# A hybrid S5 / RG-LRU encoder block: chunk matrices begun earlier and summed by accumulating transfers, a first norm by halves, half tiles for the embedding's results

## The chip, the cores and the metric

The kernel runs on one core of one Trainium2 chip. The metric is device time in microseconds of one execution, all inputs and outputs in HBM. The core has a matrix engine (PE), a vector engine (DVE), a scalar engine (ACT), GpSimd (POOL), a queue engine that issues transfers (SP) and 16 DMA engines. All of the engines run in order, each through its own list of instructions, and wait for each other by semaphores.

## The reference, cut to what matters

One layer on 1024 tokens of 1024 channels in float32. The part that the change touches is the S5 branch: `u_a`, the first 1024 columns of the in-projection, goes through a complex diagonal state space in 64 groups of 16 channels with 64 states, forwards and backwards, and a GELU.

```python
u = rms_norm(h, g_mix[l])
proj = u @ w_in[l]
u_a, x_b, gate_b, merge_a, merge_b = jnp.split(proj, SPLITS, axis=-1)
...
lam_bar = jnp.exp(lam * dt)
b_bar = ((lam_bar - 1.0) / lam)[..., None] * lax.complex(b_re, b_im)
bu = jnp.einsum('bsgh,gph->bsgp', u.astype(jnp.complex64), b_bar)
state = linear_scan(a, bu, reverse)
return jnp.einsum('bsgp,ghp->bsgh', state, c).real
...
gate_p = jax.nn.sigmoid(rms_norm(h, g_ple[l]) @ w_ple_gate[l])
h = h + gate_p * (p[l] @ w_ple_proj[l])
```

Around it stand an RG-LRU branch, a merge of both branches, an output projection `w_o`, a SwiGLU feed-forward layer of 2816 columns, and the gated embedding of the last two lines above.

## The kernel before

Every float32 product is made of three passes over pieces `h` and `l` (high and low part) of both operands: `gemm` (L159) multiplies wh·xh, wh·xl and wl·xh into one PSUM bank, 128x512 a matmul. `split` (L134, L135) makes the pieces of a weight: a cast on ACT, a subtraction on DVE.

The kernel runs through these stages, by the times of the profile:

- **First norm and transposes**, to 24 us (L190 to L221). `norm_pair` squares two tiles of 128 tokens on ACT (L194), makes their reciprocal root with two small Newton chains on DVE, and scales them (L198); then `transposed_half` transposes four tiles through PSUM (tiles `ptx`) into `xh` and `xl`, which hold the channels on the partitions.
- **In-projection of `u_a`** (`pi_u`) and the tables of the S5 part, to about 143 us.
- **The S5 stage**, to about 510 us: 16 chunks `hb` of 64 channels, `s5_step` (L635). For a chunk, `s5_mats` (L487) loads a table `tb` and makes two matrices of 128x1024 by products of broadcast columns. `mo` and `mt` are each a product, a second product goes to `mu`, and a third row adds it (L503 twice, L505). Then PE multiplies `mo` and `mt` into the PSUM tile `pk` (L516, L519); ACT copies `pk` to `kt` (L522, L523), DVE adds the skip term (L526), and `kt` goes through HBM to a matrix `m0`. PE also transposes `mt` into `pmi` (L536), which ACT copies to `mi` (L538). `s5_front` multiplies the chunk's inputs `U` by `mi` into `pS` (L551) and rotates the result into `bb`. `s5_mid` scans `bb` on DVE (L586), carries sums between blocks (tile `carry`), scans again (L610) and rotates the result into the states `X` (L614). `s5_out` multiplies `m0`·U, `mo`·X into `py` (L625 to L627) and stores its GELU.
- In the same stage the in-projections `pi_x`, `pi_g`, `pi_b`, `pi_a` (48 matmuls each) are written behind the steps by `FILL`, and PE takes them while a chunk waits.
- **LRU and branches, merge, `w_o`**, to about 1090 us; then **the feed-forward layer**, whose products `q` (L1060) are recombined by blocks and whose operand sums `s` come from weights `fu` and `ws_fg` (L1047, L1071, L982). Near 1146 us `embed_proj` (L1171) multiplies the embedding by `w_ple_proj` as filler, eight times into two banks `ppj`, copies them into one 128x1024 tile `prj` and stores it to HBM. Down projection, gate and final norm follow.

What sets the order: the program is written as Python loops, and a scheduler of the framework then puts the instructions of each engine in an order, by priority and by the time at which it thinks their operands are ready. The pools take part in this, since a tile waits for the last reader of the buffer that it gets. In the S5 stage these are: `mo` three buffers, `mt` one, `mu` one, `X` two; two PSUM buffers shared by `pk`, `pmi`, `pS` and `py`; two PSUM buffers for the `pi` tiles. Tiles from `ot` (L78) share three buffers of 128x1024: `junk`, the outputs `oi` of the in-projection, `prj`, the operand tiles of the feed-forward sums among them. 128x512 tiles of the tag `vt` have four.

`s5_step` makes matrices and fronts of chunks 0 and 1 first, then, at each step, `s5_mid` of the chunk, `s5_mats` and `s5_front` of the chunk two ahead, and `s5_out` of the chunk.

Of the kernel before, what the change touches and what calls it, by code (L numbers as in the profile page):

```python
# [53 lines left out]
def block_kernel(tc, a, out):  # L54
# [20 lines left out]
    def psb(name):  # L75
        return pb.tile([128, 1024], F32, name=name, tag="pb")
# [112 lines left out]

    def norm_pair(q):  # L190
        qs = slice(q * 2, q * 2 + 2)
        for j in range(q * 2, q * 2 + 2):
            junk = ot("junk")
            A.activation(junk, xt[j], AF.Square, bias=warm, accum_out=ss[:, j:j + 1])  # L194
        A.activation(rs[:, qs], ss[:, qs], AF.Sqrt, bias=epsc, scale=1.0 / D)
        rstd_newton(rs[:, qs], ss[:, qs], nt[:, qs])
        for j in range(q * 2, q * 2 + 2):
            V.tensor_scalar(xt[j], xt[j], rs[:, j:j + 1], None, MUL)  # L198

    def transposed_half(h):  # L200
# [3 lines left out]
        for k0 in range(0, KT, len(ks)):  # L204
# [5 lines left out]
            for k in ks:  # L210
# [3 lines left out]
                V.scalar_tensor_tensor(xl[k0 + k][:, cs], src, g, xh[k0 + k][:, cs].bitcast(F32), MUL, SUB)  # L214

    pv = psb("pv")
    T.transpose(pv[:, :8], grow, ident[:8, :8])
    V.tensor_copy(gmix, pv[:, :8])
    for h in range(2):
        norm_pair(2 * h)  # L220
        norm_pair(2 * h + 1)  # L221
        first_w[h] = split(first_w[h], [128, 8, 128], f"u{h}")
        transposed_half(h)


# [258 lines left out]
    def st5(name, bufs, shape=None):  # L484
        return s5p.tile(shape or [128, 1024], F32, name=name, tag=name, bufs=bufs)

    def s5_mats(hb):  # L487
        tb = tabp.tile([128, MATW], F32, name="tb", tag="tb", bufs=2)
# [10 lines left out]
        def gen(o1, o2, q1, q2, name):  # L499
            t = st5(name, 3 if name == "mo" else 1, [128, 8, 16, 8])  # L500
            u = st5("mu", 1, [128, 8, 16, 8])
            for dst, o, q in ((t, o1, q1), (u, o2, q2)):
                V.tensor_tensor(dst, v8(o).unsqueeze(2).to_broadcast([128, 8, 16, 8]),  # L503
                                v16(q).unsqueeze(3).to_broadcast([128, 8, 16, 8]), MUL)
            V.tensor_tensor(t, t, u, ADD)  # L505
            return t

        mo = gen(O_LA, O_LB, O_K1, O_K2, "mo")
        t = gen(O_T1, O_T2, O_B1, O_B2, "mt")

        k1 = v16(O_K1)
        pk = psb("pk")
# [4 lines left out]
        for g in range(4):  # L517
            for q in (g, 4 + g):
                T.matmul(pk[0:16, g * 128 + 112:(g + 1) * 128], bq[q], k1[:, q, :], start=(q < 4), stop=(q >= 4))  # L519
        kt = tabp.tile([16, 15, 4, 16], F32, name="kt", tag="kt", bufs=1)  # L520
        pkv = pk[0:16].rearrange("p (q n) -> p q n", q=8)
# [110 lines left out]

    sts = {}

    def s5_step(hb):  # L635
        if hb == 0:
            for q in range(2):
                sts[q] = {"m": s5_mats(q)}
            s5_front(0, sts[0])
            s5_front(1, sts[1])  # L640
        s5_mid(hb, sts[hb])
        if hb + 2 < 16:
            sts[hb + 2] = {"m": s5_mats(hb + 2)}
            s5_front(hb + 2, sts[hb + 2])
        s5_out(hb, sts.pop(hb))

# [251 lines left out]
    def half(n):  # L898
        return slice(n * 512, n * 512 + 512)
# [271 lines left out]
    def embed_proj(m):  # L1171

        if m % 4 == 0:
            with hp(HPW):
                wpp[0] = wload(a["w_ple_proj"][0][:, m * 128:m * 128 + 512], f"pp{m}")
        ps = [bank("ppj"), bank("ppj")]
        gemm(ps, wpp[0], pth, ptl, ms=slice((m % 4) * 128, (m % 4 + 1) * 128))
        yield
        t = ot("prj")
        for n in range(2):  # L1180
            A.copy(t[:, half(n)], ps[n])
        dma(prd[m], t)
        yield
# [198 lines left out]
```

## Time and profile before

| | us |
|---|---|
| median of three runs | 1907.72 |
| the three runs | 1906.96, 1907.72, 1909.06 |
| profiled execution, its own time | 1907.41 |
| its span in the trace | 1905.2 |
| PE busy | 1841.4 (97%) |
| DVE busy | 1315.1 (69%) |
| ACT busy | 909.7 (48%) |
| POOL busy | 7.8, 60 instructions |
| granted clock of PE, mean | 0.994 |

The span is the first to the last instruction of the trace; the execution's own time is 2.2 us more. PE idles 63.8 us of the span. A row of a timeline gives start, duration, engine, line of the kernel, operation, tile written and tiles read, shape, and in brackets the idle time of that engine just before the row with what ended it. Consecutive rows of a pipelined engine overlap a little, so that their spacing and not their duration is what one of them adds to a queue.

### The profile page before, as it was taken

To read this page: it belongs to the slowest core of one execution; us is meant where nothing else is said; L and a number is where in the kernel's file an instruction comes from. 1 tells how busy PE (TensorE), PEld (TensorE's weight loads), DVE (VectorE), ACT (ScalarE), POOL (GpSimd) and SP (SyncE) were. 2 spreads that over 40 slices of the span, in tenths; PEclk is the share of its full clock that TensorE was granted. 3 is DMA by queue.
4 is the path that set the end of the run, shared out by engine and by line. 5 is a ranking of instruction groups with operands and counts; after the bars stand their busy time and mean duration, and the time that the engine had idled before them with its cause. 6 is when DMAs were issued, how large, how long until landed. Compare 5 with 4: busy or idle time off the path is not lost.

```text
span 1905.2 us, 23270 instructions
## 1 busy us (share of the span) xinstructions
PE 1841.4 (97%) x8997; PEld 1532.0 (80%) x8997; DVE 1315.1 (69%) x1810; ACT 909.7 (48%) x1238; POOL 7.8 (0%) x60
## 2 busy tenths in 40 slices
PE   7999889988999999999999999999999999999998
PEld 6787777777788888878888887888888888888887
DVE  7517999999534779797444677867777774343875
ACT  6675666656555687865223454223232332122543
POOL 0000000000000000000000000000000000000000
PEclk8999999999999999999999999999999999999999
DMA  4795343433233356565746645422222264322433
GB/s 146 194 234 151 112 128 119 131 115 109 97 111 99 129 193 211 164 210 179 230 134 180 184 166 188 145 76 91 76 92 74 93 217 130 96 83 67 139 111 127
DMA packets 285855, 263.48 MB, mean 138 GB/s; under 512 B 32688, under 2 KB 244784, under 8 KB 285744
## 3 DMA queue, kind: packets, MB, share of 16 engines
q1 hardware_dynamic: 285744, 261.99, 44.2%
q8 instruction: 71, 1.16, 0.3%
q14 instruction: 40, 0.33, 0.1%
HBM read 185.86 MB, written 76.09 MB: 137 GB/s over the span
## 4 chain that ended last, share of the span: by engine, by line
PE 68%; DVE 2%; DMA 1%; ACT 1%; issue 1%; DVEq 0%; ACTq 0%
PE q L1060 22%; PE pfd L159 13%; PE pwo L159 5%; PE ppg L159 5%; PE pi_a L159 5%; PE pgl L159 5%; PE pg L159 4%; PE pbo L159 4%; PE pi_b L159 3%; PE pao L159 2%; PE ppj L159 1%; DMA ld_yb<-ybd 1%; DMA brd<-ta 1%; PE pfin L1312 0%; PE pxr L1195 0%
## 5 line engine op out<-in xcount | busy, mean ns | idle before, releaser
L1271 DVE TENSOR_TENSOR h<-h,pfd 128x512 f32<-128x512 f32 x48 | 32.6, 684 | 113.3 <-PE pfd L159 113.3
L982 ACT CAST s<-rs 128x512 fp32r<-128x512 f32 x44 | 27.2, 618 | 148.4 <-DVE rs L1072 148.4
L159 PE MATMUL pfd<-fh,wh_fd 128*128 128x512 f32 x288 | 88.7, 389 | 0.0
L159 PE MATMUL pfd<-fl,wh_fd 128*128 128x512 f32 x288 | 88.7, 389 | 0.0
L159 PE MATMUL pfd<-fh,wl_fd 128*128 128x512 f32 x288 | 88.6, 389 | 0.0
L134 ACT CAST wh_fd<-ws_fd 128x768 fp32r<-128x768 f32 x24 | 20.1, 835 | 122.1 <-PE pfd L159 121.4
L1060 PE MATMUL q<-xt2h,s 128*128 128x512 f32 x176 | 59.2, 398 | 4.3 <-ACT s L982 3.9
L159 PEld LDWEIGHTS pfd<-fl,wh_fd 128*128 128x128 f32 x288 | 54.1, 188 | 11.3
L159 PEld LDWEIGHTS pfd<-fh,wh_fd 128*128 128x128 f32 x288 | 54.1, 188 | 11.2
L159 PEld LDWEIGHTS pfd<-fh,wl_fd 128*128 128x128 f32 x288 | 54.1, 188 | 11.2
L1060 PE MATMUL q<-xt3h,s 128*128 128x512 f32 x176 | 57.7, 389 | 0.0
L1060 PE MATMUL q<-xt1h,s 128*128 128x512 f32 x176 | 57.7, 389 | 0.0
L1060 PE MATMUL q<-xt4h,a 128*128 128x512 f32 x176 | 57.7, 389 | 0.0
L1060 PE MATMUL q<-xb1h,s 128*128 128x512 f32 x176 | 57.7, 389 | 0.0
L551 PE MATMUL pS<-U,mi 128*128 128x128 f32 x256 | 32.6, 281 | 22.6 <-ACT mi L538 22.6
L551 PEld LDWEIGHTS pS<-U,mi 128*128 128x128 f32 x256 | 29.7, 191 | 28.9 <-ACT mi L538 28.5
L159 PE MATMUL pwo<-mh,wh_wo 128*128 128x512 f32 x128 | 51.5, 402 | 0.0
L159 PE MATMUL ppg<-uh,wh_pg 128*128 128x512 f32 x128 | 50.8, 397 | 0.0
L159 PE MATMUL pwo<-mh,wl_wo 128*128 128x512 f32 x128 | 50.1, 392 | 0.0
L159 PE MATMUL ppg<-uh,wl_pg 128*128 128x512 f32 x128 | 49.9, 390 | 0.0
L159 PE MATMUL ppg<-ul,wh_pg 128*128 128x512 f32 x128 | 49.8, 389 | 0.0
L159 PE MATMUL pwo<-ml,wh_wo 128*128 128x512 f32 x128 | 49.8, 389 | 0.0
(544 smaller groups left out, 5362.9 us busy)
## 6 DMA issues: line engine op xcount, KB each, us to landing
ws_fg<-in_w_ff_gate_dram SPq DMA_DIRECT2D x22, 512.0 KB, 4.2
fu<-in_w_ff_up_dram SPq DMA_DIRECT2D x22, 512.0 KB, 4.0
hid<-up SPq DMA_DIRECT2D x22, 512.0 KB, 3.4
hid<-hid SPq DMA_DIRECT2D x22, 512.0 KB, 4.6
ws_fd<-in_w_ff_down_dram SPq DMA_DIRECT2D x24, 384.0 KB, 3.5
ws_wo<-in_w_o_dram SPq DMA_DIRECT2D x16, 512.0 KB, 5.0
ws_pg<-in_w_ple_gate_dram SPq DMA_DIRECT2D x16, 512.0 KB, 3.9
tb<-tab SPq DMA_DIRECT2D x16, 384.0 KB, 3.1
```

The lines of the kernel that those rows point to most:

```text
L134: A.copy(wh, st)
L159: T.matmul(pn_[:, sub], ww[:, k0 + k, ms], xn[:, sub], start=(first and i == 0), stop=(last and i == tot - 1))
L551: T.matmul(pS[:, q * 128:(q + 1) * 128], mi[:, q, :], rhs, start=True, stop=True)
L982: A.copy(h, raw)
L1060: T.matmul(ps, ww[:, k], xx, start=i == 0, stop=i == 11)
L1271: V.tensor_tensor(hres[m][:, half(n)], hres[m][:, half(n)], ps[n], ADD)
```

## The change

There are three parts.

**S5 matrices.** `s5_mats` is split. Its loads and products become `s5_gens`, which is called for the chunk three ahead of the step (L635 of before, `s5_step`); what is left of `s5_mats` gets the finished tiles. The row on DVE that added `mu` to `mo` or `mt` (L505) is taken out. In its place GpSimd issues a transfer from `mu` to `mo` or `mt`, SBUF to SBUF, 512 KB, whose write adds to what is there (32 in all). `mu` gets two buffers. `kt` becomes a tile of the shared `ot` buffers in place of one of its own. In a step `s5_out` now stands after `s5_mats` and ahead of the next `s5_gens` and `s5_front`.

**First norm.** `norm_half` takes four tiles at once. The squares of the odd tiles move to DVE, one scaling in four moves to ACT. The zero that the second half's squares use is made from a column of `xl[4]`, so that they can't begin earlier.

**Embedding.** The result of `embed_proj` goes through two 128x512 tiles of the tag `vt`, each with its own store, and no longer through one `ot` tile.

```diff
-    def norm_pair(q):
-        qs = slice(q * 2, q * 2 + 2)
-        for j in range(q * 2, q * 2 + 2):
+    def norm_half(h, start):
+
+        qs = slice(h * 4, h * 4 + 4)
+        for j in range(h * 4, h * 4 + 4):
             junk = ot("junk")
-            A.activation(junk, xt[j], AF.Square, bias=warm, accum_out=ss[:, j:j + 1])
+            if j % 2:
+                V.tensor_tensor_reduce(junk, xt[j], xt[j], 1.0, start, MUL, ADD, ss[:, j:j + 1])
+            else:
+                A.activation(junk, xt[j], AF.Square, bias=start, accum_out=ss[:, j:j + 1])
...
-        for j in range(q * 2, q * 2 + 2):
-            V.tensor_scalar(xt[j], xt[j], rs[:, j:j + 1], None, MUL)
+        for j in range(h * 4, h * 4 + 4):
+            if j % 4 == 3:
+                A.mul(xt[j], xt[j], rs[:, j:j + 1])
+            else:
+                V.tensor_scalar(xt[j], xt[j], rs[:, j:j + 1], None, MUL)
...
-        norm_pair(2 * h)
-        norm_pair(2 * h + 1)
+        norm_half(h, zeros[h])
         first_w[h] = split(first_w[h], [128, 8, 128], f"u{h}")
         transposed_half(h)
+        if h == 0:
+
+            V.tensor_scalar(zeros[1], xl[4][:, 0:1].bitcast(F32), 0.0, None, MUL)
...
-    def s5_mats(hb):
+    def s5_gens(hb):
...
             t = st5(name, 3 if name == "mo" else 1, [128, 8, 16, 8])
-            u = st5("mu", 1, [128, 8, 16, 8])
+            u = st5("mu", 2, [128, 8, 16, 8])
...
-            V.tensor_tensor(t, t, u, ADD)
+
+            G.dma_start(out=t.rearrange("p a b c -> p (a b c)"), in_=u.rearrange("p a b c -> p (a b c)"), accum_op=ADD)
             return t
...
-
-        k1 = v16(O_K1)
+        return rb, mo, t, v16(O_K1)
+
+    def s5_mats(hb, rb, mo, t, k1):
...
-        kt = tabp.tile([16, 15, 4, 16], F32, name="kt", tag="kt", bufs=1)
+        kt = ot("kt")[0:16, 0:960].rearrange("p (m g h) -> p m g h", m=15, g=4)
...
         if hb == 0:
-            for q in range(2):
-                sts[q] = {"m": s5_mats(q)}
-            s5_front(0, sts[0])
-            s5_front(1, sts[1])
+            for q in range(3):
+                g = s5_gens(q)
+                if q < 2:
+                    sts[q] = {"m": s5_mats(q, *g)}
+                    s5_front(q, sts[q])
+            gens.append(g)
         s5_mid(hb, sts[hb])
         if hb + 2 < 16:
-            sts[hb + 2] = {"m": s5_mats(hb + 2)}
+            sts[hb + 2] = {"m": s5_mats(hb + 2, *gens.pop())}
+        s5_out(hb, sts.pop(hb))
+        if hb + 3 < 16:
+            gens.append(s5_gens(hb + 3))
+        if hb + 2 < 16:
             s5_front(hb + 2, sts[hb + 2])
-        s5_out(hb, sts.pop(hb))
...
-        t = ot("prj")
         for n in range(2):
-            A.copy(t[:, half(n)], ps[n])
-        dma(prd[m], t)
+            t = qp.tile([128, 512], F32, name="prj", tag="vt", bufs=4)
+            A.copy(t, ps[n])
+            dma(prd[m][:, half(n)], t)
```

The order of the instructions moves with this at three places. In the orders below `xN` is the count of equal instructions in a row, and a number behind a name tells tiles of one name apart.

**PE, the first chunks of the S5 stage.** `pi_x` are in-projections, `pk`, `pmi` and `pS` as above. Before, from the first chunk's `pk`:

```order
L516 MATMUL pk<-mo,mt 16x112 x8
L519 MATMUL pk<-tb,mt 16x16 x8
L536 MATMUL pmi<-ident,mt 128x128 x8
L159 MATMUL pi_x_2044<-xh_118,wh_in_x_2040 128x512 x2
L159 MATMUL pi_x_2044<-xl_126,wh_in_x_2040 128x512 x2
L159 MATMUL pi_x_2044<-xh_118,wl_in_x_2041 128x512 x2
```

And in the changed kernel, from the first chunk's `pk` to the third's:

```order
L531 MATMUL pk<-mo,mt 16x112 x8
L534 MATMUL pk<-tb,mt 16x16 x8
L551 MATMUL pmi<-ident,mt 128x128 x8
L566 MATMUL pS<-U,mi 128x128 x8
L531 MATMUL pk<-mo,mt 16x112 x8
L534 MATMUL pk<-tb,mt 16x16 x8
L551 MATMUL pmi<-ident,mt 128x128 x8
L566 MATMUL pS<-U,mi 128x128 x8
L531 MATMUL pk<-mo,mt 16x112 x8
L534 MATMUL pk<-tb,mt 16x16 x8
L551 MATMUL pmi<-ident,mt 128x128 x8
L159 MATMUL pi_x_2046<-xh_118,wh_in_x_2042 128x512 x2
```

Before, 19 matmuls of `pi_x` stood behind the first `pmi`, 5 and 15 around the first `pS` (which took two chunks at once), and 16 and 5 around the third `pmi`; now none stands until the third chunk's `pmi`.

**DVE, a step in the middle of the stage.** Rows L564 and L565 are rotations, `wl_in_g` is a weight's low part. Before:

```order
L503 TENSOR_TENSOR mo<-tb 128x1024
L602 SCALAR_TENSOR_TENSOR carry<-carry 128x64
L505 TENSOR_TENSOR mo<-mo,mu 128x1024
L607 TENSOR_TENSOR carry<-carry,rb 128x16x7
L503 TENSOR_TENSOR mu<-tb 128x1024
L608 TENSOR_TENSOR carry<-carry 128x8x7
L505 TENSOR_TENSOR mt<-mt,mu 128x1024
L609 TENSOR_TENSOR bb<-bb,carry 128x8x7
L524 TENSOR_TENSOR kt<-ident,dcol 16x64
L610 SCALAR_TENSOR_TENSOR Y<-dzf,bb 128x1024
```

And in the changed kernel:

```order
L514 TENSOR_TENSOR mu<-tb 128x1024
L601 SCALAR_TENSOR_TENSOR Y<-dzf,bb 128x1024
L579 TENSOR_TENSOR risw<-risw,rb 128x1024
L514 TENSOR_TENSOR mo<-tb 128x1024
L580 TENSOR_TENSOR bb<-pS,rb 128x1024
L614 TENSOR_TENSOR carry<-carry,rb 128x128
L584 TENSOR_TENSOR bb<-bb,risw 128x1024
L615 TENSOR_TENSOR carry<-carry 128x64
L135 TENSOR_TENSOR wl_in_g_3370<-ws_in_g_3367,wh_in_g_3369 128x1024
L617 SCALAR_TENSOR_TENSOR carry<-carry 128x64
L514 TENSOR_TENSOR mu<-tb 128x1024
```

The two additions are gone, and the products stand between the rows of other chunks. On POOL, where before only the memsets of `carry`, `dzf` and `X` (L583, L580, L613) stood, two accumulating transfers a step now stand between them, most often `mo` ahead of `carry` and `dzf`, and `mt` ahead of `X`.

**SP, the transfers around the embedding.** `prd` is the store of `prj`, `fu` a weight of the feed-forward layer. Before:

```order
L1182 DMA prd_7740<-prj 128x1024
L1106 DMA hdd_7734<-hd 128x1024
L1106 DMA hdd_7735<-hd 128x1024
L1106 DMA hdd_7736<-hd 128x1024
L1182 DMA prd_7741<-prj 128x1024
L1047 DMA fu_8999<-in_w_ff_up_dram 128x8x128
```

And in the changed kernel:

```order
L1203 DMA prd_7728<-prj 128x512 x2
L1068 DMA fu_8997<-in_w_ff_up_dram 128x8x128
L1140 DMA ru<-hdd_7720 128x1024
L1203 DMA prd_7729<-prj 128x512 x2
```

The load of `fu` now stands behind the fourth result's store and ahead of the fifth's; before, it stood behind the fifth's and three stores of `hd`.

## Rows read from the trace of the kernel before

**Rows 1.** The page's first part: busy time, share, instructions of each engine.

```profile
PE 1841.4 (97%) x8997; PEld 1532.0 (80%) x8997; DVE 1315.1 (69%) x1810; ACT 909.7 (48%) x1238; POOL 7.8 (0%) x60
```

**Rows 2.** What PE waited for: total us, times, longest.

```profile
PE pS L551 <- ACT mi L538: 22.6, 14, 1.9
PE pk L516 <- DVE mt L505: 9.6, 11, 2.2
```

**Rows 3.** Busy time by stretch: length, then each engine; PEclk; DMA share; GB/s.

```profile
core 0: us, PE busy (x) PEld busy (x) DVE busy (x) ACT busy (x) POOL busy (x), PEclk, DMA share, GB/s
...
143.00:163.00 20.00, 17.83 (x82) 14.53 (x81) 10.76 (x10) 9.16 (x10) 0.00 (x0) 1.00 0.77 212
163.00:213.00 50.00, 46.25 (x314) 39.24 (x314) 46.27 (x52) 31.59 (x41) 0.44 (x3) 1.00 0.40 123
213.00:467.00 254.00, 228.64 (x1556) 197.21 (x1557) 246.35 (x278) 160.80 (x229) 5.37 (x37) 1.00 0.39 118
467.00:510.00 43.00, 37.89 (x227) 32.48 (x226) 30.36 (x33) 24.69 (x34) 0.54 (x3) 1.00 0.26 81
```

**Rows 4.** Timeline of PE in one step, from one chunk's pk to the next's.

```profile
277.25 1.69 PE L516 MATMUL pk<-mo,mt 128*16 128x112 f32 x16 [0.94 <-DVE mt L505]
278.78 0.67 PE L519 MATMUL pk<-tb,mt 128*16 128x16 f32 x16
279.38 1.09 PE L536 MATMUL pmi<-ident,mt 128*128 128x128 f32 x8
...
284.42 2.05 PE L551 MATMUL pS<-U,mi 128*128 128x128 f32 x16 [1.65 <-ACT mi L538]
...
298.77 1.69 PE L516 MATMUL pk<-mo,mt 128*16 128x112 f32 x16 [0.96 <-DVE mt L505]
```

**Rows 5.** Timeline of DVE in the same step: the additions.

```profile
293.70 1.19 DVE L505 TENSOR_TENSOR mo<-mo,mu 128x1024 f32<-128x1024 f32 x1
...
297.40 1.22 DVE L505 TENSOR_TENSOR mt<-mt,mu 128x1024 f32<-128x1024 f32 x1
```

**Rows 6.** Timeline of ACT in the same step.

```profile
280.68 1.05 ACT L482 COPY rosw<-Y 64x1024 f32<-64x1024 f32 x1
281.75 0.98 ACT L522 COPY kt<-pk 16x448 f32<-16x448 f32 x1
282.53 0.98 ACT L523 COPY kt<-pk 16x448 f32<-16x448 f32 x1
283.32 1.04 ACT L538 COPY mi<-pmi 128x1024 f32<-128x1024 f32 x1
```

**Rows 7.** Timeline of DVE and PE where the stage begins.

```profile
156.90 1.22 DVE L503 TENSOR_TENSOR mt<-tb 128x1024 f32<-128x1024 f32 x1
158.04 1.22 DVE L505 TENSOR_TENSOR mo<-mo,mu 128x1024 f32<-128x1024 f32 x1
...
159.70 0.62 PE L159 MATMUL pi_x<-xl,wh_in_x 128*128 128x512 f32 x2
160.15 0.61 PE L159 MATMUL pi_x<-xh,wl_in_x 128*128 128x512 f32 x2
162.93 1.69 PE L516 MATMUL pk<-mo,mt 128*16 128x112 f32 x16 [2.17 <-DVE mt L505]
```

**Rows 8.** The page's DMA issues: count, KB each, median us to landing.

```profile
hid<-up SPq DMA_DIRECT2D x22, 512.0 KB, 3.4
ws_wo<-in_w_o_dram SPq DMA_DIRECT2D x16, 512.0 KB, 5.0
...
x<-in_x_dram SPq DMA_DIRECT2D x8, 512.0 KB, 8.1
```

**Rows 9.** Timelines at the embedding: SP's queue, then PE.

```profile
1150.70 0.41 SPq L1182 DMA_DIRECT2D prd<-prj  x1
1151.77 0.38 SPq L1047 DMA_DIRECT2D fu<-in_w_ff_up_dram  x1
...
1160.36 0.50 PE L1060 MATMUL q<-xt2h,s 128*128 128x512 f32 x1 [3.86 <-ACT s L982]
```

**Rows 10.** Timelines of the start: DVE, then PE.

```profile
11.77 1.23 DVE L135 TENSOR_TENSOR wl_u<-ws_u,wh_u 128x1024 fp32r<-128x1024 f32 x1 [0.24 <-ACT wh_u L134]
...
13.90 1.42 DVE L198 TENSOR_SCALAR x<-x,rs 128x1024 f32<-128x1024 f32 x2
...
21.13 0.83 PE L208 MATMUL ptx<-ident,x 128*128 128x128 f32 x4 [4.46 <-DVE xl L214]
```

More of the change, by code (lines that the diff above doesn't have):

```diff
@@ L214, in transposed_half @@
                 V.scalar_tensor_tensor(xl[k0 + k][:, cs], src, g, xh[k0 + k][:, cs].bitcast(F32), MUL, SUB)
+    zeros = [warm, cp.tile([128, 1], F32, name="zero2")]
     pv = psb("pv")
@@ L633, in block_kernel @@
     sts = {}
+    gens = []
     def s5_step(hb):
         if hb == 0:
-            for q in range(2):
-                sts[q] = {"m": s5_mats(q)}
-            s5_front(0, sts[0])
-            s5_front(1, sts[1])
+            for q in range(3):
[4 more added lines that the diff above has]
+            gens.append(g)
         s5_mid(hb, sts[hb])
         if hb + 2 < 16:
-            sts[hb + 2] = {"m": s5_mats(hb + 2)}
+            sts[hb + 2] = {"m": s5_mats(hb + 2, *gens.pop())}
[3 more added lines that the diff above has]
+        if hb + 2 < 16:
             s5_front(hb + 2, sts[hb + 2])
-        s5_out(hb, sts.pop(hb))
     xbd = [dram(f"xbd{f}", [128, 1024]) for f in range(8)]
```

## The prediction

> **What bounds the kernel now.** I read the busy times first, then what PE waited for, then the stretches, then timelines of the stretches in which PE idles. PE is busy 1841.4 us of a span of 1905.2 us [rows 1], so at most 63.8 us can be won without taking matmuls away, and the change takes none away. The list of PE's waits puts half of that in one stage: 22.6 us in 14 waits of `pS` for `mi`, 9.6 us in 11 waits of `pk` for `mt` [rows 2]. By stretch, the S5 stage idles 20.00 − 17.83 = 2.17 us at its beginning, 50.00 − 46.25 = 3.75 us in its first chunks, 254.00 − 228.64 = 25.36 us in its twelve steady steps and 43.00 − 37.89 = 5.11 us at its end [rows 3].
>
> In the steady steps DVE is as much a bound as PE. A step is 254.00 / 12 = 21.17 us. DVE is busy 246.35 / 12 = 20.53 us of it and PE 228.64 / 12 = 19.05 us [rows 3]. One step shows how they lock: `pk` begins at 277.25 and the next at 298.77, each after a wait for DVE's addition into `mt` of 0.94 and 0.96 us, with 1.65 us lost between at `pS` [rows 4]. ACT is there too: `mi` is copied at 283.32, behind two copies of `kt` and the rotation's `rosw` [rows 6].
>
> **Steady steps: the additions leave DVE.** Two additions a step go, of 1.19 and 1.22 us [rows 5]. Two products beside each other begin 1.14 us apart (156.90 and 158.04 [rows 7]), so DVE loses 2 × 1.14 = 2.3 us a step and has 18.2 us left. That is less than PE's 19.05 us, so PE would become the bound if nothing else held it. Three things will still hold it.
>
> The copy of `mi`. It begins 0.98 + 0.98 us (0.78 + 0.79 by spacing) after `kt`'s first copy and lasts 1.04 us [rows 6]; so `mi` is there 2.6 us after `pk`, and 0.85 us of that are `pmi`'s spacing (rows 4: the next matmul after `pmi`'s start at 279.38). In the new order 2 to 6 matmuls of `pi` stand between `pmi` and `pS` in the early steps, at (160.15 − 159.70) / 2 = 0.23 us each [rows 7]; in the late ones two and twelve of `py`, some 3 us. The early ones leave 0.5 us, and about 2 us more where `rosw`'s two copies come ahead, and the late ones nothing. In the late ones `py` waits for the addition into `kt` instead, as it shares the PSUM buffer of `pk`.
>
> The transfers themselves. No accumulating transfer and no transfer from POOL is in this trace. Let L be the time from the second product's end to the sum's landing. Plain transfers of the same 512 KB land 3.4 to 5.0 us after their issue, and 8.1 us where eight of them start at once [rows 8]. An accumulating one reads both tiles and passes POOL's queue, so I take L = 5 us, at the upper plain row, with 3.4 and 8.1 as ends. By the Trainium skill, "DMA: Bandwidth & Descriptors", section "Anatomy of one DMA — SWDGE (gpsimd) path", a transfer from GpSimd takes 2.0 us and its bytes over 436 GB/s: 3.2 us for 512 KB by my estimate, stated for a plain one; by that the sum below would be the second rival's, and no run has yet shown it here.
>
> The buffers. DVE's next product into `mu` must wait for the transfer that reads the buffer, and DVE is in order: in the new order some 4 us of other rows stand between, so that L = 5 stalls all that is queued behind (rotations, scans, `carry`) about 1 us, once or twice a step. 18.2 + 1.5 = 19.7 us for DVE, and with the waits at `pS` I take a step of 20.1 us: 12 × (21.17 − 20.1) = **+13 us**. Ends: +17 with 0.7 us of PE idle left a step, +3 where the stalls come twice and `rosw` always stands ahead of `mi`. On POOL the memsets of `dzf` and `X` are queued behind transfers that wait for DVE's products; these memsets, 37 rows of 5.37 us in the stretch [rows 3], are short, and what their place costs I leave within these ends.
>
> **The first chunks.** This is the price. The order shows `pk`, `pmi`, `pS` of chunk 0, then of 1, then `pk`, `pmi` of 2, with no `pi` between. The next `pi` needs a PSUM bank whose output tile waits for `kt`'s store, now in the same three buffers. So every microsecond of the transfer is bare here:
>
> - Chunk 0: the second product for `mt` takes the place of the addition at 158.04 and ends near 159.3; PE's last `pi` ends at 160.8 [rows 7]. PE idles L − 1.5 us (now 2.17).
> - Chunks 1 and 2: `mt` has one buffer, so its first product waits for `pmi`: `pk` and `pmi` 3.0 us [rows 4], the product 1.2, then L, so 4.2 + L. PE has 3.0 and `pS`'s 1.9 us in that time. L − 0.7 each.
> - Chunk 3: `mo` has three buffers, so its product waits for chunk 0's `py`, behind which 8 `pi` (1.8 us) stand ahead of `pk`: 1.2 + L − 1.8 = L − 0.6.
>
> Together 4L − 3.5, 16.5 us at L = 5, for 2.17 + 3.75 = 5.9 us today [rows 3]: **−10.6 us**. In chunks 4 to 9 the same wait of `mo` has 25 `pi` (5.7 us) for cover, which hides L up to 4.5 us; above it each step loses L − 4.5 (0.5 us at L = 5, inside the 20.1). In chunks 10 to 15 the transfers have 8 us and more of slack.
>
> **End of the stage.** Now 5.11 us idle, waits of `py` for the last `X`. In the new order only two `py` groups stand behind the last `pS`, and full in-projections between them; I leave 1.5 us: **+3.6 us** (ends +1 and +4).
>
> **Embedding.** PE waits 3.86 us at 1160.36 for the operand sum `s` made from `fu`, whose load SP issues at 1151.77, right after a store of `prj` at 1150.70 that waited for its copies [rows 9]. The change puts that load ahead of the fifth result's store. It has at least the 4 to 5 us that are missing, and the two half stores have nothing behind them that PE needs. The sums move late for the next two products instead, behind some 8 us of other `q`: **+3.8 us** (ends 0, if the next sum is late by as much, and 4.3).
>
> **Start.** Squares on two engines win some 3 us of ACT. But `wl_u` of 1.23 us, which waits for its weight until 11.77, now stands ahead of the chain for all four tiles, and the last transposes of the first half come later. PE's 4.46 us at 21.13 [rows 10] shrink, and the second half comes later by about as much. I put **0**, with −2 and +2.
>
> **Sum.** 13 − 10.6 + 3.6 + 3.8 + 0 = 9.8 us off the profiled execution's 1907.41 us, 1897.6 us; the median of the runs is 0.3 us higher, so **1898 us**. The sum hangs on L: above 4.5 us each microsecond of it costs 4 us in the first chunks and 6 us in chunks 4 to 9, and the gain is gone at L = 6.0. Below 4.5 only the 4 us count: at 3.4 it is 9.8 + 5 + 4.4 = 19 us, at 7 it is 10 us lost.
>
> **Rivals.** *The transfers are slow* (slower). One mechanism: with L of 6.4 us or more, `mo` of chunk k, which waits for `py` of chunk k − 3, lands after PE has used up its 25 `pi`. At 7 us the time is 1918. For it: accumulating reads and writes more than the plain rows do, POOL's queue mixes transfers with memsets, and 8.1 us exists [rows 8]. Against: the DMA engines are busy 0.39 of this stretch only [rows 3].
>
> *PE becomes the bound* (faster than forecast). L of 3.4 us and `mi` early: 17 − 4.2 + 3.6 + 3.8 = 20 us, 1887. For it: DVE's 18.2 under PE's 19.05. Against: the three things above.
>
> *The first chunks eat it* (no change). At L near 6, or with a second `pi` output held back by `kt`, the stage's first 60 us lose what the steady steps win: 1904 to 1911.
>
> *POOL is shut out by DVE* (slower). In this stage every large row of DVE is a TENSOR_TENSOR or a scan; a TENSOR_TENSOR of 128x1024 takes 1.2 us [rows 7], while the two TENSOR_SCALAR rows of that size at the start take 1.42 us together [rows 10], so DVE has a mode of double rate that the stage does not use. If the transfers nevertheless had to wait until DVE pauses, they would get one pause a step, as DVE idles 254.00 − 246.35 = 7.65 us in twelve [rows 3]; with 5 us lost in each of 16 chunks that is 1980. The Trainium skill, "SBUF — State Buffer", section "Summary: rules for kernel authors", says that a transfer issued by GpSimd gets no descriptors while DVE is in a 2× or 4× mode, and advises against hiding one under DVE. By that rule, read with the rows above, the stage would be safe; the rule speaks against the change only if a row here runs in such a mode.
>
> **Chances.** The forecast (1890 to 1903) 0.40; PE bound 0.20; no change 0.15; slow transfers 0.21; shut out 0.04. Runs of this kernel lie within 0.1% of each other, and about 0.2%, 3.8 us, is what a measurement can tell: faster 0.60, same 0.15, slower 0.25. The range of 8 in 10 reaches from 1881 (PE bound, with the start's +2 and the embedding's 4.3 us) to 1917 (L near 7).
>
> **What would show it.** Right: `pk` to `pk` about 20 us in the middle of the stage, no wait of `pk` for an addition, DVE near 18 us busy a step; waits of `pk` of several microseconds for a transfer in the first three chunks; transfers landing near 5 us after issue; no 3.86 us wait of `q` near 1160. Wrong: transfers of 6.5 us or more and a wait at each `pk` in the first ten chunks; `py` waiting for `X` because POOL's memset came late; a steady step still at 21 us, which would mean that DVE's additions were not what locked it.

## The result, and the profile after

The changed kernel takes 1955.96 us (median of four runs, 1950.56 to 1959.97), the kernel before 1907.84 us beside it: a ratio of 1.0251, 95% interval 1.023 to 1.0271. It is 48 us slower; 10 us less were forecast. The profiled execution took 1959.97 us with a span of 1958.2 us.

From the first part of the page of the changed kernel, its row of the queue in which GpSimd's transfers lie (packets, MB, share of 16 engines) and its rows of their issue (KB each, median us to landing):

```profile
PE 1865.5 (95%) x8997; PEld 1552.4 (79%) x8997; DVE 1289.0 (66%) x1773; ACT 909.4 (46%) x1232; POOL 35.4 (2%) x92
...
q0 software_dynamic: 4608, 16.78, 4.7%
...
mo<-mu POOLq DMA_DIRECT2D x16, 512.0 KB, 5.3
mt<-mu POOLq DMA_DIRECT2D x16, 512.0 KB, 5.4
```

Against [rows 1], DVE gave up 26.1 us. But PE idles 1958.2 − 1865.5 = 92.7 us where it idled 63.8, and the same 8997 matmuls keep it busy 24.1 us longer. 28.9 + 24.1 = 53.0 us is the whole difference of the two profiled spans. So about half of the loss is added waiting, and the other half is matmuls that took longer. This is an account of the span; it doesn't say what either half would give back if the other were gone.

Where it lies is seen by cutting both traces at the same pieces of work: the last of the u projection, the first `pk`, the fourth, the sixteenth, the first `pi_a`. Busy time by stretch, first of the kernel before, then of the changed one:

```profile
core 0: us, PE busy (x) PEld busy (x) DVE busy (x) ACT busy (x) POOL busy (x), PEclk, DMA share, GB/s
140.00:162.90 22.90, 20.77 (x99) 16.69 (x97) 10.66 (x10) 12.06 (x15) 0.25 (x3) 1.00 0.83 226
162.90:213.30 50.40, 46.33 (x315) 39.38 (x316) 46.67 (x54) 31.69 (x41) 0.44 (x3) 1.00 0.40 122
213.30:465.40 252.10, 227.03 (x1537) 195.57 (x1538) 244.45 (x276) 160.57 (x228) 5.26 (x36) 1.00 0.39 119
465.40:576.10 110.70, 105.59 (x534) 88.82 (x534) 58.81 (x58) 60.20 (x68) 0.65 (x4) 1.00 0.30 96
```

```profile
143.90:168.90 25.00, 20.76 (x98) 16.65 (x98) 9.47 (x9) 9.14 (x14) 3.00 (x6) 0.97 0.91 234
168.90:222.90 54.00, 36.08 (x241) 30.81 (x242) 41.54 (x48) 28.52 (x40) 5.06 (x10) 0.82 0.59 138
222.90:517.00 294.10, 253.29 (x1585) 215.94 (x1586) 231.43 (x257) 170.19 (x238) 25.80 (x60) 0.94 0.59 151
517.00:630.60 113.60, 111.17 (x561) 93.87 (x561) 50.61 (x49) 60.57 (x64) 0.32 (x2) 1.00 0.30 98
```

The four stretches are 436.1 us before and 486.7 us after, 50.6 us longer, with PE busy 21.6 us more in them. Most of it stands in the twelve steps: 252.1 to 294.1 us, 24.5 us a step for 21.0. But the matmul counts show that work has moved: the first chunks hold 241 matmuls where they held 315, and 48 of the 74 missing ones are done in the steps. PE's idle time has risen by 16.0 us in the first two stretches (6.2 to 22.2) and by 15.7 us in the steps (25.1 to 40.8). The granted clock, 1.00 in all four before, is 0.82 in the first chunks and 0.94 in the steps. The rest of the program is 2.4 us longer: 3.9 us before these stretches, 6.3 us won at the embedding, some 5 us of small differences in between and after.

What PE waited for in the changed kernel (us in total, times, longest):

```profile
PE pk L531 <- DMA mo<-mu: 22.3, 5, 7.1
PE py L640 <- DVE kt L541: 14.4, 7, 5.4
PE pk L531 <- DMA mt<-mu: 9.3, 3, 4.2
PE pS L566 <- ACT mi L553: 3.6, 2, 2.5
```

The waits of [rows 2] have shrunk or gone: `pS` waits 3.6 us for `mi` in place of 22.6, and no addition is waited for. In their place stand transfers, 31.6 us, and `kt`, 14.4 us, which was no wait at all before. The new waits are also longer: up to 7.1 us, where the longest of the old ones in this stage was 2.2.

### The profile page after: what moved, and what is told of

Same layout as the page of the kernel before. It is cut to its first block, busy times and chain, and to the rows that moved or that the text cites. A ratio compares the mean times of both kernels' runs of the same rounds, so it can differ in the third digit from the quotient of the medians.

```text
span 1958.2 us, 23345 instructions
## 1 busy us (share of the span) xinstructions
PE 1865.5 (95%) x8997; PEld 1552.4 (79%) x8997; DVE 1289.0 (66%) x1773; ACT 909.4 (46%) x1232; POOL 35.4 (2%) x92
## 4 chain that ended last, share of the span: by engine, by line
PE 67%; DVE 2%; DMA 2%; ACT 2%; issue 1%; SPq 0%; DVEq 0%; ACTq 0%
PE q L1081 21%; PE pfd L159 12%; PE pwo L159 4%; PE ppg L159 4%; PE pi_a L159 4%; PE pi_b L159 4%; PE pbo L159 4%; PE pg L159 4%; PE pgl L159 3%; PE pao L159 2%; PE ppj L159 1%; DMA ld_yb<-ybd 1%; DMA brd<-ta 0%; PE pfin L1333 0%; PE pxr L1216 0%
## 5 line engine op out<-in xcount | busy, mean ns | idle before, releaser
L531 PE MATMUL pk<-mo,mt 128*16 128x112 f32 x256 | 36.3, 310 | 35.6 <-DMA mo<-mu 22.3
L531 PEld LDWEIGHTS pk<-mo,mt 128*16 128x16 f32 x256 | 28.0, 121 | 44.6 <-issue 34.9
L514 DVE TENSOR_TENSOR mu<-tb 128x1024 f32<-128x1024 f32 x32 | 39.0, 1220 | 26.2 <-DMA mt<-mu 13.9
```

The lines of the kernel that those rows point to most:

```text
L531: T.matmul(pk[0:16, q * 128:q * 128 + 112], bq[q], mo[:, q, :, d:d + 7], start=True, stop=True)
```

## What a long wait does to the matmuls behind it

The longest wait, of the fourth chunk's `pk`, in PE's timeline of the changed kernel, and then its stretches of 4 us around it, with the columns as above:

```profile
222.87 3.14 PE L531 MATMUL pk<-mo,mt 128*16 128x112 f32 x16 [7.13 <-DMA mo<-mu]
```

```profile
216.00:220.00 4.00, 0.00 (x0) 0.00 (x0) 3.06 (x8) 2.81 (x6) 0.86 (x1) 0.83 0.50 116
220.00:224.00 4.00, 1.13 (x7) 0.93 (x8) 3.68 (x3) 1.70 (x3) 0.32 (x2) 0.50 0.94 212
224.00:228.00 4.00, 4.00 (x34) 3.56 (x33) 2.36 (x2) 3.05 (x4) 0.00 (x0) 0.50 0.15 24
228.00:232.00 4.00, 3.01 (x13) 1.92 (x13) 3.54 (x4) 3.02 (x3) 0.86 (x1) 0.89 0.83 300
```

PE stands still for 7.13 us; the granted clock (the third number from the end) falls to 0.50, from 2.4 to 1.2 GHz, and `pk` takes 3.14 us where it took 1.69 us in [rows 4]. The stretch from 228 is back at 0.89 on the mean. The `pk` behind the waits of 4.25, 3.48, 4.66 and 4.09 us take 3.14 to 3.15 us too, and none of the waits of the kernel before brought this on in this stage. Cut into stretches of 1 us, 52.3 us of PE's busy time in the stage lie below full clock, where none did before; at the clocks granted that is an estimated 23.6 us of extra busy time, close to the 21.6 us measured. No step of the prediction had them.

## The experiments

Each run is compared with runs of the kernel before that were taken beside it; the number given is the difference of the two medians, with the ratio and its interval.

**Additions back on DVE, all else as changed.**

```diff
-            G.dma_start(out=t..., in_=u..., accum_op=ADD)
+            V.tensor_tensor(t, t, u, ADD)
```

> The changed kernel, with its three parts and its early matrices, but the 32 sums are additions on DVE again and no transfer adds. Theory A (the transfers: some 5.4 us from issue to landing stand bare between a product and pk, and the waits bring the granted clock down): the S5 stage returns to that of before or a little better, no wait of pk over 2.5 us after the first three chunks, the granted clock of the stage back to 1.00, time 1903 to 1912. Theory B (the new order: early matrices and kt in the shared buffers make the engines, which run in order, wait for each other): still 1925 or more, with py waiting for kt and pk for DVE.

1926.21 us for 1907.07: +19.1 us, 1.0102 (1.0087 to 1.0117). The time is theory B's, 1925 or more, and so are the waits: `py` for `kt` (6.0 us), `pk` for DVE's rows (14.8 us). Theory A's 1903 to 1912 is missed by 14 us. But 48.1 − 19.1 = 29 us do go with the transfers, so both play a part, and something else in the change costs the rest.

**No sums at all.** The same place left empty; mo and mt hold one product.

> The changed kernel with neither transfers nor additions: mo and mt keep only their first product, so that the S5 outputs lack the second. It shows what the sums cost altogether in the new order. Theory A: all of the S5 loss goes and DVE's 2.3 us a step are won too: 1885 to 1898, first chunks included. Theory B: the order still locks the engines, 1915 or more.

1919.80 us, +12.7 us, 1.0069 (1.0054 to 1.0085). With nothing to add anywhere the new arrangement is still slower than the kernel before, as theory B said. Taking the additions off DVE altogether, at no price, is worth 19.1 − 12.7 = 6.4 us in this order, not the 13 us that the prediction put on the steps.

**A plain copy from SP in place of the accumulating transfer.**

```diff
-            G.dma_start(out=t..., in_=u..., accum_op=ADD)
+            dma(t..., u...)
```

> The changed kernel with each accumulating transfer of POOL replaced by a plain copy of the same 512 KB from mu to mo or mt, issued by SP: the first product is overwritten, so that mo and mt hold the second product only. Theory A1 (any transfer there costs this, since some 4 us from issue to landing are bare anyway): 1935 to 1956. Theory A2 (it is POOL's queue or the accumulation: descriptors made by software, the memsets of dzf and X behind it): landing 3.5 us, waits of pk gone, 1905 to 1920.

1921.92 us, +14.9 us, 1.0076 (1.0059 to 1.0092), 2 us above theory A2's range and far under A1's. A transfer of 512 KB at this place costs only 2 us more than nothing, when it lands after 3.2 us.

**The plain copy from POOL**, in which only the accumulation is left out; the order of every engine is the same as in the changed kernel, instruction for instruction.

```diff
-            G.dma_start(out=t..., in_=u..., accum_op=ADD)
+            G.dma_start(out=t..., in_=u...)
```

> The changed kernel word for word, with the accumulation taken out of POOL's transfers: the same 512 KB, the same queue, the same order of all engines, but a plain copy, so that mo and mt hold the second product only. Theory M (adding on the way is what makes the landing 5.4 us): landing about 3.2 to 4 us as from SP, 1920 to 1932. Theory N (POOL's path is slow, whatever the transfer does): landing 5 us or more, 1948 to 1957.

1927.13 us for 1908.80: +18.3 us, 1.0102 (1.0084 to 1.0121). The group of these transfers, of this run and then of the changed kernel (durations on POOL in ns min/median/max, first and last start; then us to landing min/median/max):

```profile
L517 POOL DMA_DIRECT2D mo<-mu x16: 527/527/667, 162.6 to 475.9; - x16
...
DMA to landing us min/median/max: 2.8/3.4/5.7
```

```profile
L517 POOL DMA_DIRECT2D mo<-mu x16: 859/859/1007, 161.6 to 506.3; - x16
...
DMA to landing us min/median/max: 4.4/5.4/8.4
```

Theory M holds. POOL's path as such is no slower than SP's (3.4 and 3.2 us); adding on the way takes 2.0 us more to landing and 0.33 us more on POOL, and the queue's share of the DMA engines is 2.3% without it and 4.7% with it. The accumulation alone costs 48.1 − 18.3 = 29.8 us of time here. Of what PE and DVE waited for, these are the transfers in this run:

```profile
PE pk L531 <- DMA mt<-mu: 3.9, 2, 2.7
PE pk L531 <- DMA mo<-mu: 3.1, 4, 1.0
DVE mu L514 <- DMA mt<-mu: 2.9, 4, 1.2
```

PE waits 7.0 us for transfers where it waits 31.6 in the changed kernel, and DVE 2.9 us where it waits 26.2 (below). Since the orders are equal, this part of the loss has its cause shown. By the Trainium skill, "DMA: Bandwidth & Descriptors", section "Anatomy of one DMA — SWDGE (gpsimd) path", 512 KB from GpSimd take an estimated 3.2 us: the plain copy's 3.4 us agree, the accumulating one's 5.4 us do not, and the measurement decides.

**Two copies from SP, one behind the other.**

```diff
+            dma(t..., u...)
             dma(t..., u...)
```

> The changed kernel with each accumulating transfer replaced by two plain copies from SP, one behind the other into the same tile, so that the tile is ready after about 6.5 us and POOL issues nothing; mo and mt hold the second product only. With one copy the time was 1921.9. Theory R (it is the time to landing that counts, each microsecond some 15 us): 1950 to 1980. Theory N (POOL's queue counts, not the landing): 1922 to 1935.

1935.47 us, +26.7 us, 1.0142 (1.0126 to 1.0158). That is 0.5 us above theory N's range, less than these runs can tell, and 14.5 us under theory R's. The second copy does cost time (26.7 − 14.9 = 11.8 us over one copy), but much less than theory R said. The orders differ: with two transfers to plan for, 35 to 47 matmuls of `pi` stand ahead of most `pk`, where 25 stand in the changed kernel's early steps. So no fixed price of a microsecond of landing follows; that it is the part which the order does not cover is read from these counts and was not tested.

**The old order with accumulating transfers**, two buffers of mu, kt in a shared buffer.

```diff
-            u = st5("mu", 1, [128, 8, 16, 8])
+            u = st5("mu", 2, [128, 8, 16, 8])
...
-            V.tensor_tensor(t, t, u, ADD)
+            G.dma_start(out=t..., in_=u..., accum_op=ADD)
...
-        kt = tabp.tile([16, 15, 4, 16], F32, name="kt", tag="kt", bufs=1)
+        kt = ot("kt")[0:16, 0:960].rearrange(...)
```

> The kernel before (old norm, old embedding, matrices two ahead and in their old place) with the sums as accumulating transfers, two buffers of mu, and kt in a shared buffer to make room for the second mu. Theory A: as slow as the S5 part of the change, 1945 to 1960, and slower than the change if being three ahead hides anything. Theory B: faster than the change, 1915 to 1935, since the old order is kept.

1970.42 us, +63.4 us, 1.0329 (1.0313 to 1.0344); theory A. The changed kernel without the embedding's share (−7.3 us, below) is at 48.1 + 7.3 = 55.4 us, so the new order of the steps, with matrices three ahead, is some 8 us better here.

**Only kt in a shared buffer.** The kernel before with the last two lines of that diff alone.

> The kernel before with one edit: kt is a tile of the three shared buffers instead of having its own. Theory B1 (the shared buffer is what costs in the new order: the outputs of the in-projections wait for kt's store, so PE has no filler between the first chunks, and kt waits for them later): 1914 to 1922, the first three pk with no pi between and a granted clock under 1 there. Theory B2 (the new order of the steps costs): 1905 to 1909, no change.

1939.69 us for 1909.63: +30.1 us, 1.016 (1.0143 to 1.0177). More than theory B1 asked, by its mechanism. Two stretches of this run, from the first `pk` to the fourth and on to the sixteenth, with the columns as above:

```profile
162.80:215.90 53.10, 33.46 (x240) 29.06 (x240) 44.35 (x51) 28.23 (x38) 0.43 (x3) 0.84 0.26 76
215.90:489.90 274.00, 244.61 (x1584) 209.83 (x1584) 249.22 (x279) 167.13 (x232) 5.37 (x37) 0.97 0.39 117
```

As B1 said, no `pi` stands between the first three `pk`, and the clock (third from the end) is 0.84 there. The first chunks hold 240 matmuls where they held 315, and PE idles 19.6 us in them for 4.1 before: with additions on DVE and no transfer at all. The steps take 22 us longer, but of that only 29.4 − 25.1 = 4.3 us are idle time; the rest is the 47 matmuls more that are now done there, some 11 us at 0.23 us each [rows 7], and the lower clock. PE waits 12.7 us for `oi_x` (4 times), a wait that the kernel before does not have. One step of ACT shows how that comes about:

```profile
292.17 0.95 ACT L522 COPY kt<-pk 16x448 f32<-16x448 f32 x1 [1.90 <-PE pk L519]
292.92 2.28 ACT L669 COPY oi_x<-pi_x 128x1024 f32<-128x1024 f32 x1
...
297.35 0.94 ACT L523 COPY kt<-pk 16x448 f32<-16x448 f32 x1
298.09 1.05 ACT L538 COPY mi<-pmi 128x1024 f32<-128x1024 f32 x1
```

An in-projection's output now stands between the two copies of `kt` and ahead of `mi`, in 8 of the 16 chunks (third to tenth); in [rows 6] the three copies follow each other. That the rotation of the shared buffers is what moved it there is read from the two orders and not tested by itself.

**Only the early order**: matrices three ahead and out ahead of the next front, kt in its own buffer, additions on DVE.

```diff
+        s5_out(hb, sts.pop(hb))
+        if hb + 3 < 16:
+            gens.append(s5_gens(hb + 3))
         if hb + 2 < 16:
             s5_front(hb + 2, sts[hb + 2])
-        s5_out(hb, sts.pop(hb))
```

> The kernel before with the new order of the steps alone: matrices begun three ahead, out ahead of the next front, but additions on DVE, one buffer of mu, kt in its own buffer, old norm and old embedding. Theory B1 (kt's buffer costs): 1903 to 1910, about no change, since mo with three buffers and mt with one can't be made earlier anyway. Theory B2 (the order costs): 1914 to 1925, with py waiting for kt, since py now takes the PSUM buffer that pk leaves.

1906.44 us for 1909.63: −3.2 us, 0.9981 (0.9972 to 0.9991). A little faster: with `kt` in its own buffer and additions on DVE, the order itself is not at fault.

**Only the embedding.**

> The kernel before with the embedding's half tiles alone. The stretch from the embedding's first matmul to the second column of the next products was 6.3 us shorter in the changed kernel. If that is this edit's own: 1900 to 1902.5. If part of it came from the other edits' shift: 1903 to 1905.

1902.37 us, −7.3 us, 0.9961 (0.9947 to 0.9976): the edit's own.

**Only the first norm.**

> The kernel before with the first norm by halves alone. In the changed kernel the u projection ends 3.9 us later. If the norm is the cause: 1910 to 1912.5, with PE waiting some 6 us for the first scaled tiles and some 5 us for xl. If something else shifts the stage (the prefetch of weights): 1906 to 1909.

1909.86 us, +0.2 us, 1.0003 (0.9994 to 1.0012): nothing that can be measured. PE's waits at the start in this run, new ones in place of the 4.5 us of [rows 10]:

```profile
PE ptx L215 <- DVE x L205: 5.9, 1, 5.9
PE pi_u L159 <- DVE xl L221: 4.7, 1, 4.7
```

**Early order, own kt, one buffer of mu, accumulating transfers.**

> The kernel with the early order and kt in its own buffer (1906.4 us with additions on DVE), now with accumulating transfers and one buffer of mu; old norm, old embedding. It shows what the transfers cost where kt is out of the way and some 40 matmuls of pi stand ahead of each pk. Theory P (two causes that feed each other: kt takes PE's filler away, and only then does a landing of 5.4 us stand bare): 1900 to 1912, no long wait of pk after the first three chunks. Theory Q (the transfers cost by themselves, since DVE in its order waits for mu's buffer): 1925 to 1945, DVE waiting 40 us or more for mu.

1974.91 us for 1909.09: +65.8 us, 1.0343 (1.0327 to 1.0359). Theory P falls: with `kt` out of the way, and 41 matmuls ahead of most `pk`, the transfers still cost 65.8 + 3.2 = 69 us against the same kernel with additions. Theory Q has the mechanism, DVE waiting 47 us for `mu`, but asked for 30 us less. Its waits, of PE and of DVE:

```profile
PE pk L521 <- DMA mt<-mu: 64.7, 15, 7.2
...
DVE mu L504 <- DMA mo<-mu: 30.7, 13, 4.1
```

With one `mu`, the two transfers of a chunk follow each other: DVE can write the second product for `mt` only when `mo`'s sum has landed, and `pk` waits for both. DVE, in its order, holds all else back meanwhile.

**The same with a plain copy from SP.**

> As the run before, but with a plain copy of 512 KB issued by SP in place of the accumulating transfer: mo and mt hold the second product only. Theory P: 1895 to 1905, since DVE's additions are gone and 3.2 us to landing are hidden. Theory Q: 1910 to 1925. The difference to the run before is what a landing of 5.4 instead of 3.2 us costs.

1913.73 us (1907.34 to 1915.61), +4.6 us, 1.0022 (1.0011 to 1.0033). Above theory P's range and inside Q's. Against the same kernel with additions it is 7.8 us slower, with transfers that land after 2.9 us; with those of the run before, which land after 5.0 us, it is 61 us more.

**Accumulating transfers, two of mu, own kt**; the room comes from m0 and U.

```diff
-        m0 = tabp.tile([128, 4, 16, 8], F32, name="m0", tag="m0", bufs=3)
+        m0 = tabp.tile([128, 4, 16, 8], F32, name="m0", tag="m0", bufs=2)
...
-        U = tabp.tile([128, 4, 128], F32, name="U", tag="U", bufs=3)
+        U = tabp.tile([128, 4, 128], F32, name="U", tag="U", bufs=2)
```

> The changed kernel, accumulating transfers and two buffers of mu, with kt in its own buffer again; the room comes from m0 and U, two buffers each in place of three, which also puts pS behind more of the matmuls. Theory K (kt's place in the shared buffers costs as much as the transfers): 1920 to 1935. Theory T (the transfers alone make the loss once they are there): 1945 to 1965.

1952.49 us, +43.7 us, 1.0225 (1.0207 to 1.0242). That is inside theory T's range, but it settles nothing, since a new wait came with the smaller pools and is as large as the gain that was looked for:

```profile
PE pS L566 <- DMA U<-ud: 21.2, 12, 6.0
```

**Idle matmuls in the waits.**

```diff
+        for i in range(12 if hb < 10 else 0):
+            T.matmul(pk[:, 0:512], xh[i % 8][:, 0:128], xh[i % 8][:, 0:512], start=True, stop=True)
```

> The changed kernel with 12 idle matmuls of 128x512 (2.7 us) ahead of each of the first ten pk, written to the bank that pk then overwrites: 27 us of work added on PE where it waits for transfers. Theory C (the granted clock that falls in long waits costs up to 21 us of its own): the clock of the stage rises from 0.93 to 0.98 or more and the time falls, 1930 to 1950. Theory D (the low clock only fills time that PE would wait anyway): clock up, time 1953 to 1965.

1974.24 us, +65.2 us, 1.0343 (1.0329 to 1.0357): 17 us slower than the change, above both ranges, with the mean clock hardly up (0.981 for 0.978). The added work moved the order of the real matmuls too (`py` then waits 20.7 us for `mi`), so it does not tell what the low clock costs in time; that PE was busy longer rests on the busy times alone, and how much shorter the kernel would be at full clock stays open.

**Early order and embedding together**, additions on DVE, own kt, old norm.

> The early order with kt in its own buffer and additions on DVE, and the embedding's half tiles; old norm. Both parts were faster alone, by 3.6 and 7.3 us of the medians of their call. They lie in different stages, so they should add: 10 to 11 us under the kernel before, 1896.5 to 1900.

1901.64 us for 1909.09: −7.5 us, 0.9959 (0.9946 to 0.9971). Faster than both kernels, but no faster than the embedding alone: the 3 us of the order do not show. The interval of this run, some 2.4 us to either side, and those of the two parts leave open whether they were lost.

## Why the prediction was wrong

**The size of the transfer was nearly right, the price of it was not.** L was taken as 5 us, from plain transfers to and from HBM; no row bore on an adding one, so that it came close is luck. It is 5.4 us at the first chunk, from the second product's end to `pk`:

```profile
162.33 1.22 DVE L514 TENSOR_TENSOR mu<-tb 128x1024 f32<-128x1024 f32 x1
...
168.91 3.14 PE L531 MATMUL pk<-mo,mt 128*16 128x112 f32 x16 [4.25 <-DMA mt<-mu]
```

In the first chunks the sum said 4L − 3.5 = 16.5 us of idle time ahead of the first four `pk`; the trace has 4.25, 3.48, 1.54 and 7.13, together 16.4 us. That this agrees is luck too: the parts were 3.5, 4.3, 4.3 and 4.4. And other waits stand in the same stretches, so that PE lost 16.0 us there and not 10.6.

**The step that failed first is the steady steps: +13 us forecast, 42 us lost** (21.0 to 24.5 us a step). Of the 42 us, 15.7 are idle time and 26.3 busy time. Some 11 us of the latter are the 48 matmuls that moved here from the first chunks (at 0.23 us each [rows 7]), and the rest is mostly the clock. Three terms of the step were mis-sized. DVE's relief was put at 2.3 us a step as if DVE alone set the pace; DVE gave up 27.5 us in the stage, 1.7 us a chunk, and with the sums left out altogether the time falls by 6.4 us in all. The wait of `mo` in chunks 4 to 9 was put at L − 4.5, 0.5 us a step; the six `pk` there wait 3.2 us on the mean, four of them for `mo`'s transfer. The last of the four, with the `py` that frees the buffer:

```profile
356.49 0.39 PE L642 MATMUL py<-X,mo 128*128 128x128 f32 x2
358.42 1.20 DVE L514 TENSOR_TENSOR mo<-tb 128x1024 f32<-128x1024 f32 x1
359.92 0.86 POOL L517 DMA_DIRECT2D mo<-mu  x1 [2.86 <-DVE mo L514]
366.65 3.15 PE L531 MATMUL pk<-mo,mt 128*16 128x112 f32 x16 [4.09 <-DMA mo<-mu]
```

The forecast counted 1.2 us for the product and L. It left out that DVE, in its order, begins the product only 1.5 us after `py` (1.5 to 3.2 us in the four cases), and from issue to `pk` it is 6.7 us here (5.0 to 7.5).

The third term is the stalls behind `mu`, put at 1 to 1.5 us a step. The waits of DVE in the changed kernel, and one such stall:

```profile
DVE mu L514 <- DMA mt<-mu: 13.9, 9, 2.3
DVE mu L514 <- DMA mo<-mu: 12.3, 9, 3.5
```

```profile
290.49 1.23 DVE L514 TENSOR_TENSOR mu<-tb 128x1024 f32<-128x1024 f32 x1 [3.51 <-DMA mo<-mu]
291.63 0.24 DVE L624 TENSOR_TENSOR bb<-bb,carry 128x56 f32<-128x56 f32 x1
291.91 2.29 DVE L625 TENSOR_TENSOR_SCAN Y<-dzf,bb 128x1024 f32<-128x1024 f32 x1
```

The product of the next chunk, which nobody needs for microseconds, waits 3.51 us for its buffer, and the carry and the scan of the chunk in hand stand behind it. Such waits make 26.2 us in the stage, 1.6 us a chunk, so their size was nearly right; the price was not. What stands behind leads to `X`, `X` is waited for by `py`, and `py` frees `mo`'s buffer for the next transfer. The forecast priced the stall of DVE and the wait of `pk` as if one covered the other; read along this chain they follow each other, which is argued from the rows and was not tested by itself.

**The second is `kt`'s buffer.** The prediction saw that `kt` in the shared buffers takes away the filler of the first chunks, but it priced that by the transfer, as bare microseconds of L. The missing filler costs without any transfer: 19.6 us of idle time in the first chunks for 4.1, and 30.1 us in all, in the old order. In the new one, the changed kernel with additions (+19.1 us) and the early order with the embedding (−7.5 us) differ in `kt`, the second `mu` and the norm: 26.6 us. Here too most of the idle time is in the first chunks, 14.5 us for 1.6. What the shared buffer did to the steps, an output ahead of `mi` on ACT, had no term at all. What the second `mu` does by itself was not run.

**The third is the clock,** for which the prediction had no term. It took PE's 1841.4 us of busy time as fixed and priced a wait of 4 us at 4 us. In the changed kernel PE is busy 21.6 us longer in the stage, with matmuls at 1.2 GHz behind its waits.

**Parts and sum.** The early order and the embedding together −7.5, `kt`, the second `mu` and the norm +26.6, the transfers over additions +29.0: 48.1 us, which is the difference measured. (Each term is the step from one run to the next, so the sum closes by construction; what is independent is that `kt` costs 30.1 and the transfers, with the second `mu`, 63.4 − 30.1 = 33.3 us in the old order too. How `kt`'s part arises inside the engines' orders is in part argued.)

**What held.** The rival of slow transfers named the mechanism, `mo` behind `py` of three chunks earlier, with the early steps at a price above L = 4.5, and half of its sign, a wait at each of the first ten `pk`, came; but it put +10 us on L = 7, and at 5.4 us the loss was already 29. The range's lower end of 1881 does not come out of the terms given for it, 1887 − 2 − 0.5 = 1884.5. The shut-out of POOL by DVE did not come: plain copies from POOL land about as fast as from SP (3.4 and 3.2 us), though DVE is busy for 86% of the twelve steps of that run, as the rows without a double-rate mode had suggested. The Trainium skill, "SBUF — State Buffer", section "Summary: rules for kernel authors", names DVE's 2× and 4× modes alone where it speaks of a transfer issued by GpSimd, and no run here tries one under such a mode. The idle time at the end of the stage fell by 2.7 us for the 3.6 forecast (110.70 − 105.59 = 5.1 us before, 113.60 − 111.17 = 2.4 us after). The norm was 0 as forecast. The embedding's direction was right and its size low, 7.3 for 3.8 us. The last `ppj` of the kernel before, and then the queue of SP and PE's start on the products, in timelines of the changed kernel:

```profile
1155.88 0.61 PE L159 MATMUL ppj<-pth,wl_pp 128*128 128x512 f32 x2
```

```profile
1202.41 0.38 SPq L1068 DMA_DIRECT2D fu<-in_w_ff_up_dram  x1
...
1214.31 0.62 PE L159 MATMUL ppj<-pth,wl_pp 128*128 128x512 f32 x2
1214.77 0.39 PE L1081 MATMUL q<-xt2h,s 128*128 128x512 f32 x1
```

The first load of `fu` is issued 12 us ahead of the last `ppj`, where it was 4 us (1155.88 − 1151.77 [rows 9]), and `q` follows `ppj` without a gap. The wait of 3.86 us [rows 9] and one of 0.42 are gone. Behind them, before, the first column of `q` kept PE busy 69.9 us of 70.3, and now it takes 68.0 with no wait: some 2 us of the gain are matmuls that no longer run at a lower clock (0.98 before, 1.00 now, in that stretch).

## What to carry to other kernels

A tile that moves into a shared set of buffers is an edit to the order of every engine that writes such tiles; count, in the new orders, what work is left for each engine to do while it waits, before pricing anything else. Take work off a busy engine by a transfer only where its landing, measured for that kind of transfer, is covered at each place where its result or its source buffer is waited for, and count on an in-order engine all that stands behind the waiting row and all that stands ahead of the row that is waited for. Look at the granted clock behind PE's long waits: here the `pk` behind waits of 3.5 to 7.1 us took nearly twice as long, which such a wait's own length doesn't show.

## What the runs showed that was not expected

An accumulating transfer of 512 KB within SBUF lands 5.4 us after its issue (4.4 to 8.4), the plain one from the same queue 3.4 us (2.8 to 5.7), and it keeps POOL 0.86 us for 0.53 and the DMA engines twice as long (4.7% and 2.3% of the span). PE's granted clock fell to 0.50 in a wait of 7.1 us and stayed there for the first microseconds of the work behind it; in this stage of the kernel before, with waits up to 2.2 us, it stayed at 1.00. And a tile of 60 KB that gave up its own buffer cost 30.1 us, most of its idle time not where the tile is waited for but where PE had no other work left.
